# Pools for the first attention loads, joined attention outputs and stores, and pools for the output projection's first tiles, in a two-layer hybrid transformer

## The chip, the cores and the metric

The program runs on one core of a Trainium2 chip. The metric is device time in microseconds (us) of one execution, lower is better; the median over several executions stands for a kernel. One further execution is taken with the hardware profiler on.

## What is computed

Two layers of a diffusion backbone over 2048 latent tokens (a grid of 32 rows by 64 columns) and 256 context tokens, width 1024. Per layer, cut to what matters here:

```python
qa, ka, va, bx, bb, bc, qn, kn, vn = _split_last(h @ w_in[l], IN_SPLITS)
o_a = windowed_gqa_latent(rope(qa), rope(ka), va, ka_c, va_c, attn_sink[l])  # 6 heads on 2 kv heads, |dt| <= 128, context, sink
o_b = gated_short_conv(bx, bb, bc, conv_w[l])
o_c = neighbourhood_attention_latent(qn, kn, vn, kn_c, vn_c, na_rpb[l])      # 6 heads, 8 x 16 window, position bias, context
x_mid = ln_affine(ALPHA * x + g1 * (concat(o_a, o_b, o_c) @ w_out[l]), ln1_g[l], ln1_b[l])
x = ln_affine(ALPHA * x_mid + g2 * expert_choice_ffn(modulate(ln(x_mid))), ln2_g[l], ln2_b[l])
```

In layer 0 the context tokens pass through the same steps (their queries see the context keys alone); in layer 1 only their keys and values are needed. Head size is 64; all is float32, and every product is made of three matmuls on operands that are split into a high and a low part.

## The kernel before

A layer is four phases, each a function: `phase_in` (L510, modulation, layer norm, projection), `phase_att` (L901), `phase_out` (L1263, output projection, norm, router) and the experts. A phase opens its pools of tiles where the pools of the phase before have been closed, so a tile's first use waits for the last use of what lay at the same place. Weights go through a stream of their own, `W`: a raw tile is loaded (L163, SP queue), ScalarE makes the high part `wh` (L178), VectorE the low part `wl` (L186). The order of the work on each engine is the order in which the program is written, with generators that are stepped in turn.

`phase_in` works on chunks of four token tiles, of which the fifth (chunk 4, after chunks 0 to 3) has two. For each it makes the q and k of the windowed heads with rotary (`a_rest`, L757), v, then q and k of the neighbourhood heads (`c_rest`) and the short convolution (L679 to L731). High and low parts of q and k (tiles `sth`, `stl`, two buffers each) go to DRAM arrays QA, KA, QC, KC. These are laid out head by head, high and low under each head, so a tile of two heads (128 partitions) is stored by two DMAs of 64 partitions for each part: `a_rest` has eight stores to a token tile (L792, L793), `c_rest` four to a piece (L665), all on the SP queue. Between the pieces of chunk 4 stand rows of the modulation (L468 on VectorE, L469 on PE).

`phase_att` takes two kv heads of the windowed attention (A: 16 latent blocks of 128 queries, 3 q heads each; in layer 0 also two context blocks) and then six neighbourhood heads (C: 4 blocks of 16 columns; in layer 0 one block of context). A block's queries are loaded by three DMAs (L983, L987), keys of a head by one (L958). Each member of a block (a q head, or a quarter of a C block) goes through: logits (PE, L1068 and L1069), maximum with mask or bias (VectorE, L1090), exp (ScalarE, L1098), transposes (PE, L1115 and L1138), high part (ScalarE, L1227), low part (VectorE, L1218), and the product with v (PE, L1173). A block ends with a copy (ScalarE, L1179), transposes (PE, L1186), a copy (L1189), and on VectorE: the sink term (L1181, A only, with an exp on ScalarE in L1182), its addition to the sum (L1191, A only), the reciprocal (L1193), the sum of the two halves (L1195) and the multiplication with the reciprocal (L1198). Then `o` is stored: MIXA by one DMA (L1200), MIXC by four (L1206), the last block's by the POOL queue. The order inside a step is written out by hand (`ORDERA`, `ORDERC`, L47 and L48), the product with v trails by three members (`LAG`). GpSimd (POOL) builds the biases of the next C block (L1020 to L1032).

`phase_out` loads for each token tile `mix` (L1284 from MIXA, L1294 from MIXC) and the convolution's parts `mh`, `ml` (L1288), transposes `mix` (L1307), splits it (L1309, L1311) and multiplies by w_out (L1324). The SP queue runs in order: a DMA that waits for a buffer holds all behind it. Eight semaphores rotate over the DMAs of SP and ScalarE.

## Time and profile before

| | before |
|---|---|
| median of 3 runs | 4099.59 us (4097.3 to 4102.42) |
| the profiled execution, own time | 4102.85 us |
| its span in the profile | 4101.1 us |
| PE busy | 3784.8 us, 92% of the span |
| VectorE (DVE) busy | 2898.5 us, 71% |
| ScalarE (ACT) busy | 2005.5 us, 49% |
| GpSimd (POOL) busy | 711.5 us, 17% |

The span is first to last instruction; 1.75 us of the profiled execution lie outside. The first layer's attention runs from 616 to 1050 us, the second's from 2705 to 3104. Busy shares are means over phases that have different limits, so each phase is read by itself.

### The profile page before, as it was taken

Reading aid. Unit: us, or ns where it says so; the run is one execution under the profiler, and the core shown is the slowest. Engines: PE = TensorE matmul, PEld = TensorE weight load, DVE = VectorE, ACT = ScalarE, POOL = GpSimd, SP = SyncE. Lnnn points to the kernel's source line nnn. Section 1 sums busy time; section 2 is a strip of 40 time slices with the busy share of each in tenths; the row PEclk is TensorE's granted clock in tenths of the full one; section 3 lists DMA queues with packets and bytes.
Section 4 is the critical chain, followed back from the end, with each engine's and each line's share of the span. In section 5 each row is a group of like instructions: output and inputs, shape, how many; then the busy total and the mean of one; then the engine's idle time right before and its main releaser. Section 6 shows DMA issues by size and latency. Waiting matters only on the chain. (4 is left out here: it accounts for less than half of the span.)

```text
span 4101.1 us, 64178 instructions
## 1 busy us (share of the span) xinstructions
PE 3784.8 (92%) x22980; PEld 3241.1 (79%) x22980; DVE 2898.5 (71%) x5836; ACT 2005.5 (49%) x3918; POOL 711.5 (17%) x658
## 2 busy tenths in 40 slices
PE   7999999999898899999996999989998965999983
PEld 5887888888787378988985888889997855999972
DVE  6555558999677477777756766469996776777765
ACT  4344338988433044444433434359884332444453
POOL 0000000022132023233311100000221321222214
PEclk9999999999999999999998999999999977999996
DMA  7666665377643777777756766553676424888875
GB/s 228 174 210 197 197 187 146 97 174 183 211 159 122 212 240 218 218 218 214 207 167 221 229 194 196 174 167 108 150 175 230 162 106 153 247 247 254 254 236 183
DMA packets 768951, 785.81 MB, mean 192 GB/s; under 512 B 144912, under 2 KB 650520, under 8 KB 766584
## 3 DMA queue, kind: packets, MB, share of 16 engines
q1 hardware_dynamic: 732776, 657.53, 53.4%
q0 software_dynamic: 34704, 123.13, 10.8%
q8 instruction: 182, 2.98, 0.3%
q14 instruction: 137, 1.12, 0.1%
q10 hardware_dynamic: 1152, 1.05, 0.1%
HBM read 603.05 MB, written 178.48 MB: 191 GB/s over the span
## 5 line engine op out<-in xcount | busy, mean ns | idle before, releaser
L178 ACT CAST wh<-wraw 128x1024 fp32r<-128x1024 f32 x636 | 656.5, 1049 | 379.8 <-DMA wraw<-in_w_in 139.0
L186 DVE TENSOR_TENSOR wl<-wraw,wh 128x1024 fp32r<-128x1024 f32 x636 | 751.2, 1216 | 17.9 <-ACT wh L178 17.5
L1218 DVE TENSOR_TENSOR pl<-pt,ph 128x256 fp32r<-128x256 f32 (+2 forms) x792 | 360.4, 495 | 13.8 <-ACT ph L1227 7.9
L632 PE MATMUL gem<-hh,wh 128*128 128x512 f32 (+1 forms) x960 | 352.5, 367 | 0.1
L1098 ACT ACTIVATE p<-lg,mx 128x640 f32<-128x640 f32 (+3 forms) x408 | 332.0, 814 | 37.5 <-DVE mx L1090 35.7
L634 PE MATMUL gem<-hh,wl 128*128 128x512 f32 (+1 forms) x960 | 348.2, 363 | 0.0
L633 PE MATMUL gem<-hl,wh 128*128 128x512 f32 (+1 forms) x960 | 346.7, 361 | 0.0
L1227 ACT CAST ph<-pt 128x256 fp32r<-128x256 f32 (+2 forms) x792 | 309.0, 446 | 58.5 <-PE pt L1115 52.5
L1838 PE MATMUL pu<-xh,wh 128*128 128x288 f32 (+1 forms) x1024 | 303.1, 296 | 8.7 <-DVE sa L1666 8.7
L1838 PE MATMUL pa<-xh,wh 128*128 128x288 f32 (+1 forms) x1024 | 299.6, 293 | 0.7 <-DVE modc L424 0.7
L1068 PE MATMUL lg<-k,q 128*128 128x384 f32 (+2 forms) x768 | 280.4, 387 | 19.5 <-DMA maskA<-in_maskA 7.4
L1840 PE MATMUL pa<-xh,wl 128*128 128x288 f32 (+1 forms) x1024 | 296.0, 289 | 0.8 <-DVE wl L186 0.8
L1839 PE MATMUL pa<-xl,wh 128*128 128x288 f32 (+1 forms) x1024 | 295.6, 289 | 0.0
L1840 PE MATMUL pu<-xh,wl 128*128 128x288 f32 (+1 forms) x1024 | 295.3, 288 | 0.0
L1839 PE MATMUL pu<-xl,wh 128*128 128x288 f32 (+1 forms) x1024 | 295.1, 288 | 0.0
L1577 POOL DMA_INDIRECT xe<-H,ix x80 | 164.4, 2055 | 475.5 <-DVE ix L1572 398.6
L1700 POOL DMA_INDIRECT ACC<-y,ix x62 | 129.9, 2094 | 576.1 <-DVE y L1681 323.6
L1069 PE MATMUL lg<-k,q 128*128 128x256 f32 x816 | 228.7, 286 | 0.3 <-ACT p L1098 0.3
L1875 PE MATMUL py<-wh,gh 128*128 128x512 f32 x512 | 206.4, 403 | 18.4 <-ACT gh L1668 11.8
L810 PE MATMUL gem<-wh,hh 128*128 128x512 f32 x544 | 219.7, 404 | 1.2 <-ACT hh L601 1.2
L811 PE MATMUL gem<-wl,hh 128*128 128x512 f32 x544 | 216.1, 397 | 1.4 <-DVE wl L186 1.4
L812 PE MATMUL gem<-wh,hl 128*128 128x512 f32 x544 | 215.7, 396 | 0.0
(346 smaller groups left out, 9680.7 us busy)
## 6 DMA issues: line engine op xcount, KB each, us to landing
wraw<-in_w_in SPq DMA_DIRECT2D x160, 512.0 KB
wraw<-in_w_gate SPq DMA_DIRECT2D x128, 512.0 KB
wraw<-in_w_up SPq DMA_DIRECT2D x128, 512.0 KB
wraw<-in_w_down SPq DMA_DIRECT2D x128, 512.0 KB
wraw<-in_w_mod SPq DMA_DIRECT2D x88, 512.0 KB
vw<-VS SPq DMA_DIRECT2D x192, 128.0 KB
q<-QA SPq DMA_DIRECT2D x204, 96.0 KB
VS<-vs SPq DMA_DIRECT2D x36, 512.0 KB
```

Source lines behind the costliest of these rows:

```text
L178: self.nc.scalar.copy(h, self.raw[i])
L186: self.nc.vector.tensor_tensor(e[1], self.raw[i], e[0].bitcast(F32), op=ALU.subtract)
L632: P.matmul(pg[:, t0:nt], wh[:, cs_], hh[:, k, t0:nt], start=(k == 0), stop=False)
L633: P.matmul(pg[:, t0:nt], wh[:, cs_], hl[:, k, t0:nt], start=False, stop=False)
L634: P.matmul(pg[:, t0:nt], wl[:, cs_], hh[:, k, t0:nt], start=False, stop=(k == KD - 1))
L1068: P.matmul(pl[:, w0:512], q[:, x, m, :], win(k), start=(x == 0), stop=(x == 1))
L1098: S.activation(p[:, 0:768 - w0], rec["lg"][:, w0:768], AF.Exp, bias=st[b]["mx"][:, m:m + 1], scale=-1.0, accum_out=st[b]["ss"][:, m:m + 1])
L1218: V.tensor_tensor(view(st[b]["pl"]), src, view(st[b]["ph"].bitcast(F32)), op=ALU.subtract)
L1227: S.copy(view(st[b]["ph"]), src)
L1838: P.matmul(pp[f], wh[:, cs_], xh[:, kk, :], start=(kk == 0), stop=False)
L1839: P.matmul(pp[f], wh[:, cs_], xl[:, kk, :], start=False, stop=False)
L1840: P.matmul(pp[f], wl[:, cs_], xh[:, kk, :], start=False, stop=(kk == KD - 1))
```

## The change

1. QA, QC and KC are laid out part by part (high, low), then head by head, so a 128-partition tile is one store: four stores to a token tile in `a_rest`, two to a piece in `c_rest`. A head's keys are now loaded by two DMAs. In all, SP and ScalarE issue 2254 DMAs instead of 2544.
2. Pools: in `phase_in` the ring `hT` becomes `hodd` and `heven`, and the PSUM tiles `gem` get a pool. In `phase_att` nearly every tile has its own pool, in an order by which the first block's q, k, mask and v lie where tiles of earlier chunks were.
3. Outputs of up to four A blocks, or of two C blocks, share one tile for maximum, sum, reciprocal and `o`. The steps L1181, L1182, L1191, L1193, L1198 and the store run once per group. The multiplication of A moves to GpSimd.
4. In `phase_out` the tiles `mix`, `mh`, `ml` of the first three token tiles get pools that lie where the last head's work has nothing; PSUM is split in three pools.

```diff
-    QA = dr("QA", [6, 2, 64, TT])
+    QA = dr("QA", [2, 6, 64, TT])
     KA = dr("KA", [2, 2, 64, TT])
-    QC = dr("QC", [6, 2, 64, TT])
-    KC = dr("KC", [6, 2, 64, TT])
+    QC = dr("QC", [2, 6, 64, TT])
...
-        hp = es.enter_context(tc.tile_pool(name="hT", bufs=2))
+        hodd = es.enter_context(tc.tile_pool(name="hodd", bufs=1))
+        heven = es.enter_context(tc.tile_pool(name="heven", bufs=1))
         sb = es.enter_context(tc.tile_pool(name="in_sb", bufs=2))
         last = l == DEPTH - 1
-        hT = {-1: [hp.tile([128, KD, 512], F32R, name=z) for z in ("hh", "hl")]}
+        hT = {}
...
+        psg = es.enter_context(tc.tile_pool(name="in_psg", bufs=4, space=PSUM))
...
                 dst = QC[l] if f < 3 else KC[l]
                 for a, z in enumerate((sh, sl)):
-                    for b in range(2):
-                        SY.dma_start(dst[2 * (f % 3) + b, a, :, tok + t0:tok + nt],
-                                     z.bitcast(F32)[64 * b:64 * b + 64, t0:nt])
+                    SY.dma_start(dst[a, 2 * (f % 3):2 * (f % 3) + 2, :, tok + t0:tok + nt].rearrange("h d n -> (h d) n"),
+                                 z.bitcast(F32)[:, t0:nt])
...
                 for a, o in enumerate((qh, ql)):
-                    for b in range(2):
-                        z = o.bitcast(F32)[64 * b:64 * b + 64]
-                        SY.dma_start(QA[l][b::2, a, :, tk].rearrange("f p n -> p f n"), z[:, 0:3, :])
-                        SY.dma_start(KA[l][b, a, :, tk], z[:, 3, :])
+                    SY.dma_start(QA[l][a, :, :, tk].rearrange("(f b) p n -> (b p) f n", b=2), o.bitcast(F32)[:, 0:3, :])
+                    SY.dma_start(KA[l][a, :, :, tk].rearrange("h d n -> (h d) n"), o.bitcast(F32)[:, 3, :])
...
-        kp = es.enter_context(tc.tile_pool(name="at_k", bufs=2))
+        def pool(name, bufs=1, **kw):
+            return es.enter_context(tc.tile_pool(name=name, bufs=bufs, **kw))
+        qp = pool("at_q")
         shift(es, 64)
-        qp = es.enter_context(tc.tile_pool(name="at_q", bufs=1))
-        vwp = es.enter_context(tc.tile_pool(name="at_vw", bufs=3))
-        op = es.enter_context(tc.tile_pool(name="at_o", bufs=6))
-        mp = es.enter_context(tc.tile_pool(name="at_m", bufs=1))
-        vp = es.enter_context(tc.tile_pool(name="at_v", bufs=2))
-        sm = es.enter_context(tc.tile_pool(name="at_s", bufs=4))
-        pp = es.enter_context(tc.tile_pool(name="at_p", bufs=3))
+        kp = [pool("at_k0")]
+        mp = pool("at_m")
+        vp = [None, pool("at_v1")]
+        vp[0] = pool("at_v0")
+        pp = pool("at_p", 3)
+        sm = pool("at_s", 3)
+        hp = [pool("at_h0")]
+        lp = [pool("at_w0")]
+        hp.append(pool("at_h1"))
+        lp.append(pool("at_w1"))
         shift(es, 64)
-        hp = es.enter_context(tc.tile_pool(name="at_h", bufs=2))
-        wp = es.enter_context(tc.tile_pool(name="at_w", bufs=2))
-        bp = es.enter_context(tc.tile_pool(name="at_b", bufs=1))
-        psl = es.enter_context(tc.tile_pool(name="at_l", bufs=2, space=PSUM))
-        pst = es.enter_context(tc.tile_pool(name="at_t", bufs=3, space=PSUM))
-        pso = es.enter_context(tc.tile_pool(name="at_po", bufs=1, space=PSUM))
+        kp.append(pool("at_k1"))
+        op = pool("at_o", 3)
+        bsp = pool("at_bias")
+        tp = pool("at_toep", 2)
+        vwp = pool("at_vw", 3)
+        vxp = pool("at_vx", 2)
+        wp = pool("at_ot", 2)
+        bp = pool("at_b")
+        psl = [pool("at_l0", space=PSUM)]
+        pst = pool("at_t", 3, space=PSUM)
+        pso = pool("at_po", space=PSUM)
+        psl.append(pool("at_l1", space=PSUM))
...
+        group = {}
+        for kind, u in [("A", 0), ("A", 1)] + [("C", u) for u in range(6)]:
+            for rows in (range(2, 6), range(6, 10), range(10, 14), range(14, NT), (0, 1)) if kind == "A" else (
+                    ((4,), (0, 1), (2,), (3,)) if u == 5 else ((4,), (0, 1), (2, 3))):
+                for j, n in enumerate(rows):
+                    group[kind, u, n] = ((kind, u, rows[0]), j, len(rows))
...
-            src = (KA if kind == "A" else KC)[l][u].rearrange("a d n -> (a d) n")
-            k = r["k"] = kp.tile([128, TT], F32R, name="k")
+            src = (KA if kind == "A" else KC)[l][:, u]
+            k = r["k"] = kp[ulist.index((kind, u)) % 2].tile([128, TT], F32R, name="k")
...
-                SY.dma_start(k.bitcast(F32)[:, 128 * t0:128 * t1], src[:, 128 * t0:128 * t1])
+                for a in range(2):
+                    SY.dma_start(k.bitcast(F32)[64 * a:64 * a + 64, 128 * t0:128 * t1], src[a, :, 128 * t0:128 * t1])
...
-                st[b] = {z: sm.tile([128, 4], F32, name=z) for z in ("mx", "ss", "rs")}
+                g, j, ng = group[b]
+                if j == 0:
+                    st["of", g] = {z: sm.tile([128, 12], F32, name=z)[:, 0:ng * nm] for z in ("mx", "ss", "rs")}
+                st[b] = {z: x[:, j * nm:j * nm + nm] for z, x in st["of", g].items()}
...
-            if kind == "A":
-                V.tensor_tensor(rec["rs"][:, :nm], sink[:, 3 * u:3 * u + 3], rec["mx"][:, :nm], op=ALU.subtract)
-                S.activation(rec["rs"][:, :nm], rec["rs"][:, :nm], AF.Exp, scale=-1.0)
+            g, j, ng = group[b]
+            of = st["of", g]
+            end = j == ng - 1
+            if end and kind == "A":
+                V.tensor_tensor(of["rs"].rearrange("p (b m) -> p b m", b=ng),
+                                sink[:, None, 3 * u:3 * u + 3].to_broadcast([128, ng, 3]),
+                                of["mx"].rearrange("p (b m) -> p b m", b=ng), op=ALU.subtract)
+                S.activation(of["rs"], of["rs"], AF.Exp, scale=-1.0)
...
-            o = op.tile([128, 4, 64], F32, name="o")
-            S.copy(o[:, :nm, :], px[:, :nm, 64:128])
+            if j == 0:
+                of["o"] = op.tile([128, 12, 64], F32, name="o")[:, 0:ng * nm, :]
+            all_ = of["o"]
+            o = all_[:, j * nm:j * nm + nm, :]
+            S.copy(o, px[:, :nm, 64:128])
+            if end and kind == "A":
+                V.tensor_tensor(of["ss"], of["ss"], of["rs"], op=ALU.add)
+            yield
+            if end:
+                V.reciprocal(of["rs"], of["ss"])
+            yield
+            V.tensor_tensor(o, px[:, :nm, 0:64], o, op=ALU.add)
+            del st[b], blks[b]
+            if not end:
+                return
+            yield
+            yield
+            (G if kind == "A" else V).tensor_tensor(all_, all_, of["rs"][:, :, None].to_broadcast([128, ng * nm, 64]),
+                                                       op=ALU.mult)
+            n0 = g[2]
             if kind == "A":
-                V.tensor_tensor(rec["ss"][:, :nm], rec["ss"][:, :nm], rec["rs"][:, :nm], op=ALU.add)
-            yield
-            V.reciprocal(rec["rs"][:, :nm], rec["ss"][:, :nm])
-            yield
-            V.tensor_tensor(o[:, :nm, :], px[:, :nm, 0:64], o[:, :nm, :], op=ALU.add)
-            yield
-            yield
-            V.tensor_tensor(o[:, :nm, :], o[:, :nm, :], rec["rs"][:, :nm, None].to_broadcast([128, nm, 64]), op=ALU.mult)
-            if kind == "A":
-                SY.dma_start(MIXA[l][128 * n:128 * n + 128, 192 * u:192 * u + 192], o[:, 0:3, :].rearrange("p m d -> p (m d)"))
+                SY.dma_start(MIXA[l][128 * n0:128 * (n0 + ng), 192 * u:192 * u + 192].rearrange("(b p) c -> p b c", p=128),
+                             all_.rearrange("p (b m) d -> p b (m d)", b=ng))
             elif n == 4:
-                SY.dma_start(MIXC[l][0:256, 64 * u:64 * u + 64].rearrange("(m p) d -> p m d", p=128), o[:, 0:2, :])
+                SY.dma_start(MIXC[l][0:256, 64 * u:64 * u + 64].rearrange("(m p) d -> p m d", p=128), all_)
             else:
                 dst = MIXC[l][256:TT, 64 * u:64 * u + 64].rearrange("(m a g b) d -> m g a b d", m=4, a=8, g=4)
-                for m in range(4):
-                    (G if b == blist[-1] else SY).dma_start(dst[m, n], o[:, m, :])
-            del st[b], blks[b]
+                for x in range(ng):
+                    for m in range(4):
+                        (G if b == blist[-1] else SY).dma_start(dst[m, n0 + x], all_[:, 4 * x + m, :])
+            del st["of", g]
...
+        yp = es.enter_context(tc.tile_pool(name="out_y", bufs=1))
+        mp = [es.enter_context(tc.tile_pool(name=f"out_m{j}", bufs=1)) for j in range(3)]
         sb = es.enter_context(tc.tile_pool(name="out_sb", bufs=2))
         rows = es.enter_context(tc.tile_pool(name="out_rows", bufs=1))
-        ps = es.enter_context(tc.tile_pool(name="out_ps", bufs=2, space=PSUM))
+        pst = es.enter_context(tc.tile_pool(name="out_pt", bufs=2, space=PSUM))
+        ps = es.enter_context(tc.tile_pool(name="out_ps", bufs=1, space=PSUM))
+        pso = es.enter_context(tc.tile_pool(name="out_po", bufs=2, space=PSUM))
         last = l == DEPTH - 1
...
-            m = sb.tile([128, 768], F32, name="mix", bufs=3)
+            m = mp[n % 3].tile([128, 768], F32, name="mix")
...
-            mh = sb.tile([128, KD, 128], F32R, name="mh", bufs=3)
-            ml = sb.tile([128, KD, 128], F32R, name="ml", bufs=3)
+            mh = mp[n % 3].tile([128, KD, 128], F32R, name="mh")
+            ml = mp[n % 3].tile([128, KD, 128], F32R, name="ml")
```

Where this moves instructions. The SP queue, stores of one token tile of chunk 4 (first layer, `a_rest`), before and now:

```order
L792 DMA QA_80<-sth 64x3x128
L793 DMA KA_82<-sth 64x128
L792 DMA QA_80<-sth 64x3x128
L793 DMA KA_82<-sth 64x128
L792 DMA QA_80<-stl 64x3x128
L793 DMA KA_82<-stl 64x128
L792 DMA QA_80<-stl 64x3x128
L793 DMA KA_82<-stl 64x128
```

```order
L792 DMA QA_80<-sth 128x3x128
L793 DMA KA_82<-sth 128x128
L792 DMA QA_80<-stl 128x3x128
L793 DMA KA_82<-stl 128x128
```

The last store of a `sth` buffer moves from the fourth place to the second, that of an `stl` buffer from the eighth to the fourth.

VectorE in the steady part of A, one block of three members; before, and now in a block that does not end its group:

```order
L1195 TENSOR_TENSOR o<-pt,o 128x192
L1218 TENSOR_TENSOR pl<-pt,ph 128x3x128
L1218 TENSOR_TENSOR pl<-pt,ph 128x2x128
L1090 ISA lg,mx<-lg,maskA,sinks 128x640
L1090 ISA mx 128x1
L1198 TENSOR_TENSOR o<-o,rs 128x192
L1181 TENSOR_TENSOR rs<-sinks,mx 128x3
L1218 TENSOR_TENSOR pl<-pt,ph 128x3x128
L1218 TENSOR_TENSOR pl<-pt,ph 128x2x128
L1090 ISA lg,mx<-lg,maskA,sinks 128x640
L1090 ISA mx 128x1
L1191 TENSOR_TENSOR ss<-ss,rs 128x3
```

```order
L1228 TENSOR_TENSOR o<-pt,o 128x192
L1258 TENSOR_TENSOR pl<-pt,ph 128x3x128
L1258 TENSOR_TENSOR pl<-pt,ph 128x2x128
L1113 ISA lg,mx<-lg,maskA,sinks 128x640
L1113 ISA mx 128x1
L1258 TENSOR_TENSOR pl<-pt,ph 128x3x128
L1258 TENSOR_TENSOR pl<-pt,ph 128x2x128
L1113 ISA lg,mx<-lg,maskA,sinks 128x640
L1113 ISA mx 128x1
L1258 TENSOR_TENSOR pl<-pt,ph 128x3x128
L1258 TENSOR_TENSOR pl<-pt,ph 128x2x128
```

The multiplication, the sink term, the addition and (below the piece) the reciprocal are gone from three blocks of four. A group's multiplication stands on GpSimd as `L1234 TENSOR_TENSOR o<-o,rs 128x768`: eight of these in each layer, and two of 384 in layer 0.

ScalarE where attention ends and the projection begins (layer 0; behind "waits" stand the semaphores, DMAHW those of SP and ScalarE DMAs, DMASW those of the POOL queue), before and now:

```order
L1179 COPY ot<-po 128x512 [waits PE_49]
L1189 COPY o<-pt 128x256 [waits DMAHW2_49,DMAHW1_49,DMAHW3_49,DMAHW0_49,PE_49]
L178 CAST wh<-wraw 128x1024 [waits DVE_49,Activation_49,Pool_49]
L178 CAST wh<-wraw 128x1024
L1309 CAST mh<-pt 128x384 [waits DMAHW1_49,DMAHW0_49,DMAHW2_49,DMASW7_49,DMAHW3_49,DMASW6_49,DMAHW4_49,DMASW5_49,DMAHW5_49,DMASW0_49,DMAHW6_49,DVE_49,DMAHW7_49,PE_49,Activation_49]
```

```order
L1203 COPY ot<-po 128x512 [waits PE_49]
L1221 COPY o<-pt 128x256 [waits DMAHW7_49,PE_49]
L178 CAST wh<-wraw 128x1024 [waits DMAHW1_49,DMAHW0_49,DMAHW2_49,DMASW7_49,DMAHW3_49,DMASW6_49,DMAHW4_49,DMASW5_49,DMAHW5_49,DMASW0_49,DMAHW6_49,DVE_49,DMAHW7_49,Activation_49,Pool_49]
L178 CAST wh<-wraw 128x1024
L1354 CAST mh<-pt 128x384 [waits PE_49] x2
```

The wait for all stores of the last head has moved from the first `mix` load and the first `mh` to the first `wh` of w_out.

## Rows read from the trace of the kernel before

**Rows 1.** Stretch of the A part, layer 0: us, busy PE, PEld, DVE, ACT, POOL, PEclk, DMA share, GB/s.

```profile
640.00:700.00 60.00, 60.00 (x425) 55.55 (x424) 59.52 (x181) 54.60 (x159) 0.00 (x0) 1.00 0.47 141
```

**Rows 2.** Timeline, chunk 4 of layer 0: start, duration, engine, instruction, idle before and releaser.

```profile
580.22 0.61 SPq L793 DMA_DIRECT2D KA<-sth  x1
...
582.88 0.60 SPq L793 DMA_DIRECT2D KA<-stl  x1
...
583.41 0.37 ACT L653 CAST sth<-gem 128x256 fp32r<-128x256 f32 x1 [3.29 <-DMA KA<-sth]
...
585.01 0.42 DVE L655 TENSOR_TENSOR stl<-gem,sth 128x256 fp32r<-128x256 f32 x1 [4.57 <-DMA KA<-stl]
...
585.66 0.37 PE L469 MATMUL tr<-ident,mcols 128*24 128x128 f32 x1 [6.13 <-DVE mcols L468]
```

**Rows 3.** Timeline where projection ends and attention begins, layer 0; last row layer 1.

```profile
607.72 1.19 SPq L665 DMA_DIRECT2D KC<-stl  x2
616.38 1.93 SPq L983 DMA_DIRECT2D q<-QA  x3
...
617.74 0.36 ACTq L731 DMA_DIRECT2D OB<-stl  x1
...
623.49 0.55 PE L1068 MATMUL lg<-k,q 128*128 128x256 f32 x1 [7.15 <-DMA k<-KA]
...
625.11 0.76 DVE L1090 CUSTOM_DVE_ANT_0 lg<-lg,maskA,sinks 128x512 f32<-128x512 f32 x1 [7.40 <-DMA maskA<-in_maskA]
...
625.96 0.69 ACT L1098 ACTIVATE p<-lg,mx 128x512 f32<-128x512 f32 x1 [4.05 <-DVE mx L1090]
...
2715.08 1.28 ACT L1098 ACT_TABLE_LOAD   x1 [8.97 <-DMA q<-QA]
```

**Rows 4.** Timeline of VectorE in a block of A, layer 0.

```profile
699.73 0.35 DVE L1198 TENSOR_TENSOR o<-o,rs 128x192 f32<-128x192 f32 x1
700.00 0.15 DVE L1181 TENSOR_TENSOR rs<-sinks,mx 128x3 f32<-128x3 f32 x1
700.07 0.88 DVE L1218 TENSOR_TENSOR pl<-pt,ph 128x384 fp32r<-128x384 f32 x2
```

**Rows 5.** Timeline of PE in the same block.

```profile
700.74 0.38 PE L1138 MATMUL pt<-ident,p 128*128 128x128 f32 x2
701.05 0.44 PE L1068 MATMUL lg<-k,q 128*128 128x384 f32 x1
...
703.11 0.38 PE L1138 MATMUL pt<-ident,p 128*128 128x128 f32 x2
703.25 0.42 PE L1068 MATMUL lg<-k,q 128*128 128x384 f32 x1
```

**Rows 6.** Timeline of POOL and VectorE where a bias is built beside A, layer 0.

```profile
755.97 3.32 POOL L1032 TENSOR_TENSOR bias<-maskC,toep 128x384 f32<-128x384 f32 x3
...
757.13 1.22 DVE L1181 TENSOR_TENSOR rs<-sinks,mx 128x3 f32<-128x3 f32 x1
```

**Rows 7.** Waits of PE in C, layer 0, 850 to 1030 us: total, times, longest.

```profile
PE po L1173 <- ACT ot L1179: 3.9, 5, 0.8
PE pt L1138 <- DVE pl L1218: 2.3, 5, 0.5
```

**Rows 8.** Timeline where attention ends and the output projection begins, layer 0.

```profile
1046.17 2.40 SPq L1206 DMA_DIRECT2D MIXC<-o  x4
1054.55 0.34 SPq L1284 DMA_DIRECT2D mix<-MIXA  x1
...
1049.22 1.99 ACT L178 CAST wh<-wraw 128x1024 fp32r<-128x1024 f32 x2
1058.69 0.48 ACT L1309 CAST mh<-pt 128x384 fp32r<-128x384 f32 x1 [7.48 <-DMA mh<-OB]
...
1057.74 0.87 PE L1307 MATMUL pt<-ident,mix 128*128 128x128 f32 x3 [8.82 <-DMA ml<-OB]
...
1059.86 1.20 PE L1324 MATMUL po<-wh,mh 128*128 128x512 f32 x2
```

More of the change, by code (lines that the diff above doesn't have):

```diff
@@ L384, in build, with mod_piece @@
     mod_done = set()
-    def mod_piece(l, j, ps, sb, split=True, big="gem", nbig=4, small="tr", apart=False, room=None):
-        pm = ps.tile([128, 512], F32, name=big, bufs=nbig)
+    def mod_piece(l, j, ps, sb, split=True, big="gem", nbig=4, small="tr", apart=False, room=None, acc=None):
+        pm = (acc or ps).tile([128, 512], F32, name=big, bufs=nbig)
         n = 4 if split else 2
@@ L524, in prep @@
             ts = chunk_tiles(c)
-            hT[c] = [hp.tile([128, KD, 512], F32R, name=z) for z in ("hh", "hl")]
+            hT[c] = [(hodd if c % 2 else heven).tile([128, KD, 512], F32R, name=z) for z in ("hh", "hl")]
             groups = GROUPS[l] if c == 0 else [(b, 2, b * DELAY) for b in range(0, len(ts), 2)]
@@ L628, in s_piece @@
                 wh, wl = W.next(key)
-                pg = ps.tile([128, 512], F32, name="gem", bufs=4)
+                pg = psg.tile([128, 512], F32, name="gem")
                 for k in range(KD):
@@ L804, in one_tile @@
                     wait_for(c, j)
-                    pg = ps.tile([128, 512], F32, name="gem", bufs=4)
+                    pg = psg.tile([128, 512], F32, name="gem")
                     for k in range(KD):
@@ L818, in ctx_tiles @@
                     wait_for(c, 1)
-                    pg = ps.tile([128, 512], F32, name="gem", bufs=4)
+                    pg = psg.tile([128, 512], F32, name="gem")
                     for k in range(KD):
@@ L866, in phase_in @@
             for j in range(8):
-                next(mod_piece(0, FIRST[j], ps, mb, j % 2 == 1))
+                next(mod_piece(0, FIRST[j], ps, mb, j % 2 == 1, acc=psg))
                 T.tick()
@@ L924, in phase_att @@
         maskC = bp.tile([128, 3 * MWID], F32, name="maskC")
-        biases = [None, bp.tile([128, BWID], F32, name="bias")]
+        biases = [None, bsp.tile([128, BWID], F32, name="bias")]
         sink = sinks[:, l, :]
@@ L1054, in qk @@
             q = blks[b]["q"]
-            pl = psl.tile([128, 1024], F32, name="lg")
+            pl = psl[i % 2].tile([128, 1024], F32, name="lg")
             w0 = 512
@@ L1304, in tr @@
             for f in parts:
-                pt = ps.tile([128, 4, 128], F32, name="pt")
+                pt = pst.tile([128, 4, 128], F32, name="pt")
                 for j in range(3):
@@ L1347, in rest @@
             yield STEP
-            y = sb.tile([128, D], F32, name="y", bufs=3)
+            y = yp.tile([128, D], F32, name="y", bufs=3)
             for h in range(2):
@@ L1390, in rest @@
             yield STEP
-            lt = sb.tile([2 * NE, 128], F32, name="lt")
+            lt = yp.tile([2 * NE, 128], F32, name="lt", bufs=2)
             V.tensor_copy(lt, pr[:, 0:128])
@@ L1395, in rest @@
             P.matmul(pl[:, NE * i:NE * i + NE], lt, two, start=True, stop=True)
-        po = [ps.tile([128, D], F32, name="po") for _ in range(2)]
+        po = [pso.tile([128, D], F32, name="po") for _ in range(2)]
         for k in range(5):
@@ L1408, in phase_out @@
         SY.dma_start(wr32, k8(t["w_router"][l]))
-        wr = rows.tile([128, KD, 2 * NE], F32R, name="wr")
+        wr = yp.tile([128, KD, 2 * NE], F32R, name="wr")
         two = rows.tile([2 * NE, NE], F32, name="two")
@@ L1429, in phase_out @@
             if n >= 2:
-                po.append(ps.tile([128, D], F32, name="po"))
+                po.append(pso.tile([128, D], F32, name="po"))
             half = 4 if n >= 2 else 6
```

34 lines of the change are left out of this document (18 added, 16 removed).

## The prediction

> **What bounds the kernel now.** I read the busy shares by engine first, then the table of stretches, then for each place that the change touches the timeline and the list of waits, always asking what ends the idle time last. PE is busy for 92% of the span, so the kernel is a PE kernel with holes, and a change gains what it closes of the holes or, where another engine sets PE's pace, what it takes off that engine. The reader is to see four kinds of place.
>
> At three joints PE stands still. In chunk 4 of the projection it waits 6.13 us for a small copy on VectorE, which stands behind L655, and this one waits for the landing of the store KA<-stl [rows 2]. Where attention begins PE waits 7.15 us for the first keys: SP issued nothing between the last store at 607.72 + 1.19 and the first q load at 616.38, the moment at which the last projection matmul ended (623.49 - 7.15 = 616.34), because q's place was still in use [rows 3]. Where attention ends PE waits 8.82 us for `mix`, `mh`, `ml`, whose loads SP could issue only at 1054.55 [rows 8]. Layer 1 repeats all three.
>
> In the A part PE is busy for 60.00 of 60 us and VectorE for 59.52 [rows 1]: both are full, and which of them sets the pace has to be read from a block. PE's starts show it: between the transposes L1138 and the logits that follow lie 0.31 us at 700.74 and 0.14 at 703.11 [rows 5], so 0.17 us in a block is a wait that the busy time hides. It stands right behind VectorE's multiplication and sink term [rows 4]. VectorE sets the pace there, but PE has little left to win.
>
> In C no engine is full; PE's waits in 180 us of it are 3.9 us for ScalarE and 2.3 for VectorE, none for a DMA [rows 7].
>
> **The sum, term by term.** It is made against the profiled execution, 4102.85 us, which is 3.26 us above the median of the runs.
>
> *Chunk 4, -5 us.* SP's spacing is (582.88 - 580.22) / 4 = 0.66 us a store [rows 2]. The last store of `sth` goes from fourth to second place, 1.3 us earlier, that of `stl` from eighth to fourth, 2.7 earlier. L653 then starts near 582.1, L655 near 582.4 instead of 585.01, PE near 583.1 instead of 585.66: 2.6 us, in two layers 5. Bounds: if a 128-partition store is that much slower to land, 1 us a layer is left; more than the hole of 6.13 it cannot give. Taken: -5, between -2 and -12. In the other chunks the saved issues give nothing, since PE runs through.
>
> *Attention's start, -14 us.* The q load now asks only for transposes long done, and k for chunk 3's matmuls, so SP issues them behind the last KC store. That store is itself one DMA instead of two, and ends near 607.7 + 0.6 = 608.3. From issue to the first logits it took 623.49 - 616.38 = 7.1 us, to the mask 625.11 - 616.38 = 8.7 [rows 3]; one more issue for k adds 0.6. So keys are there at 616.0 and the mask near 617.6, both when PE ends the projection or little after. The next late thing is ScalarE: its last OB store ends at 617.74 + 0.36 = 618.10, then a table load of 1.28, so the first exp starts near 619.4 instead of 625.96: 6.6 us. In layer 1 the table load began 8.97 us after ScalarE's last work, at 2715.08; behind two OB issues (0.9 us by estimate, from 0.36 for one and the gap between them) it would begin 8.1 earlier. Sum 14.7; I take 14, as OB's issues may wait about a microsecond for a semaphore that the early loads hold. Bounds: -8 if the loads, beside the last stores, land 3 us later than they did alone; -17 if the table load falls into time in which ScalarE is idle anyway.
>
> *A part, -11 us.* In three blocks of four VectorE loses L1181 (700.00 to 700.07: 0.07) and its like L1191 and L1193 (taken at 0.07 each), in every block L1198 (699.73 to 700.00: 0.27) [rows 4]: 0.27 + 3/4 x 0.21 = 0.43 us a block. There are 64 latent blocks in the two layers: 28 us if VectorE alone sets the pace. PE's visible wait is 0.17 a block, 11 us. I take PE's value, since PE cannot run faster than its own instructions; the ends are 3 (a quarter of it) and 28. ScalarE loses only L1182 in three of four.
>
> GpSimd gets 18 multiplications. A 384-wide one takes 3.32 / 3 = 1.1 us [rows 6], so 768 is 2.2 by estimate. Nothing but a store waits for them: a group's output tile comes round again three groups later. What they can do is hold VectorE up: L1181, an operation of 0.15 us on three columns took 1.22 beside a GpSimd operation [rows 6]. [...] I count it at nothing, because the operations that are stretched in the row stand once per group now, and behind a group's multiplication comes a block without them [rows 4, 6]; what fills VectorE there, L1090 and L1218, reads PSUM.
>
> *C part, -3 us.* The two-block groups take one reciprocal and the fixed part of one multiplication from each pair. Of PE's 6.2 us of waits in 180 [rows 7] half may go in the first layer, little in the second. Bounds: -6 (all of the first layer's) and +3 (stores of eight at once, which hold q and v loads longer).
>
> *Output projection's start, -5.5 us.* The loads no longer wait: they issue behind SP's last store, at 1046.17 + 2.40 = 1048.57 instead of 1054.55, 6 us earlier [rows 8]. But the wait for the last head's stores has gone to ScalarE's first `wh` of w_out. Before, both casts lay hidden at 1049.22 [rows 8]. Now they begin when the last stores have landed, at 1054.55, where SP's load was released; 1.99 for both and 0.48 for `mh` [rows 8] put the first product near 1057.1 instead of 1059.86. That is 2.8 us a layer. Bounds: -2 in all if the POOL queue's stores land 2 us later than SP's release shows; -12 if the casts too wait for nothing.
>
> Sum: -5 - 14 - 11 - 3 - 5.5 = -38.5: the profiled execution near 4064, the median near 4099.6 - 38.5 = 4061.
>
> **The rivals.**
> - *VectorE alone sets A's pace* (28 for A, 6 for C): -58.5, 4041. For it: 59.52 of 60 [rows 1]. Against: PE's own wait is 0.17 [rows 5].
> - *A's pace does not move*, since ScalarE or PE's own chain follows at once (3 for A, 0 for C): -27.5, 4072. For it: PE 60.00 of 60 [rows 1].
> - *The first loads still wait*, as some pool lies differently than read: without attention's start and with nothing in the output projection but its own shift, -5 - 11 - 3 = -19, 4081.
> - *GpSimd locks VectorE out*: 16 x 2.2 + 2 x 1.1 = 37 us lost in A, so -1, 4098: no difference. For it: the stretched L1181 [rows 6]. [...]
> - *C's stores block its loads*: slower. There are 22 bursts of eight stores in the two layers; four more stores in a row hold SP for 2.4 us [rows 8]. If q and v loads had no lead over their use, each burst would cost PE that: 22 x 2.4 = 53, in all +14, 4114. It decides from the point at which the lead is under 2.4 us; no DMA among PE's waits [rows 7] speaks against it.
>
> **How the numbers follow.** Forecast 0.48 (alone it would be 4050 to 4070), A's pace unmoved 0.22, VectorE alone 0.12, loads still waiting 0.08, GpSimd 0.05, stores 0.05. The range runs from 4037, just below the case of VectorE alone, to 4082, above the case of waiting loads, and leaves out the last two and the far ends. A measurement of this kernel can tell about 0.2%, 8 us: the first four cases are faster, 0.90; GpSimd is no difference, 0.05; stores are slower, 0.05.
>
> **What would show it.** In the profile after: PE's hole in chunk 4 near 3.6 us; q loads issued before the last projection matmul and the first exp near 3.3 us after it; A's blocks 0.17 us shorter, with the pair of starts at L1138 as close after the first member as after the second; the multiplications on GpSimd without stretched operations on VectorE; `wh` of w_out cast some 5 us later than before, and the first product 2.8 us earlier. It is wrong if PE waits for q or v in C, if the first exp comes over 6 us after the last projection matmul, or if A's block time does not change.

## The result, and the profile after

The changed kernel is slower. Its median is 4132.94 us (4129.18 to 4136.26, 4 runs) against 4101.01 of the kernel before (4 runs): a ratio of 1.0072, 95% interval 1.0059 to 1.0086. The forecast was 4061, faster by 0.9%. The profiled execution took 4129.18 us, its span is 4127.4, 26.3 us more than before. The page's first lines:

```profile
span 4127.4 us, 63392 instructions
...
PE 3797.2 (92%) x22980; PEld 3245.8 (79%) x22980; DVE 2870.0 (70%) x5574; ACT 2004.1 (49%) x3868; POOL 732.2 (18%) x676
```

VectorE has 28 us less to do, as the joining promised, and nothing came of it. To see where the time went I cut both traces at the same events: a layer's last projection matmul, the transposes of the first output (L1186, in the changed kernel L1215), those of A's last block, those of the last C block, and the first and last product of the output projection (L1324, now L1369). Lengths in us, layer 0 and layer 1:

| stage | before | after | difference, both layers |
|---|---|---|---|
| projection | 508.9, 457.2 | 507.9, 455.1 | -3.1 |
| its end to the first output | 23.1, 25.1 | 16.4, 16.2 | -15.6 |
| A, first to last output | 187.0, 176.3 | 184.4, 173.7 | -5.2 |
| C, from there to the last output | 222.5, 195.6 | 238.2, 222.4 | +42.5 |
| last output to first product | 11.2, 11.4 | 12.6, 13.4 | +3.4 |
| output projection | 246.1, 218.9 | 249.6, 220.8 | +5.4 |
| all else | | | -1.1 |

The sum is +26.3. The first three gain 24 us; C alone loses 42.5.

**Attention's start** (timelines of the changed kernel; the last row is layer 1) answers to [rows 3]:

```profile
599.78 1.99 SPq L1003 DMA_DIRECT2D q<-QA  x3
...
617.42 1.28 ACT L1121 ACT_TABLE_LOAD   x1 [1.11 <-DVE stl L729]
618.72 0.69 ACT L1121 ACTIVATE p<-lg,mx 128x512 f32<-128x512 f32 x1
...
2714.26 0.69 ACT L1121 ACTIVATE p<-lg,mx 128x512 f32<-128x512 f32 x1
```

SP issues the first q 16.6 us earlier, and the first exp starts 3.6 us after the last projection matmul (615.13) instead of 9.9. **Chunk 4** answers to [rows 2]; the hole is 4.74 us instead of 6.13, and PE goes on 2.1 us earlier:

```profile
582.90 0.43 DVE L658 TENSOR_TENSOR stl<-gem,sth 128x256 fp32r<-128x256 f32 x1 [3.47 <-DMA KA<-stl]
...
583.56 0.37 PE L470 MATMUL tr<-ident,mcols 128*24 128x128 f32 x1 [4.74 <-DVE mcols L469]
```

**A** answers to [rows 1, 5]. VectorE is down from 59.52 to 57.72 us in 60, PE is as full as before, and the wait of 0.31 us between L1162 and the logits L1088 is still there. The stretch, then PE, then ScalarE in the same block:

```profile
640.00:700.00 60.00, 60.00 (x427) 55.42 (x426) 57.72 (x147) 54.33 (x153) 4.43 (x3) 1.00 0.52 138
```

```profile
692.92 0.38 PE L1162 MATMUL pt<-ident,p 128*128 128x128 f32 x2
693.23 0.44 PE L1088 MATMUL lg<-k,q 128*128 128x384 f32 x1
```

```profile
692.28 0.81 ACT L1121 ACTIVATE p<-lg,mx 128x640 f32<-128x640 f32 x1
692.97 0.21 ACT L1121 ACTIVATION_READ_ACCUMULATOR p<-lg,mx 128x1 f32 x1
```

The logits start 0.05 us after ScalarE has read out the sum of an exp (692.97 + 0.21 = 693.18), which frees one of two tiles of logits. Before the change it was the same 0.05 us: 700.79 + 0.21 = 701.00, and the logits of [rows 5] start at 701.05.

```profile
700.79 0.21 ACT L1098 ACTIVATION_READ_ACCUMULATOR p<-lg,mx 128x1 f32 x1
```

With the multiplication gone from VectorE the wait is as long as before, so it was not VectorE's multiplication that the logits waited for. A block fell from 5.69 to 5.66 us.

**C** in layer 1. VectorE's waits from 2905 to 3120 us, then GpSimd's (total, times, longest):

```profile
DVE lg L1113 <- POOL bias L1052: 12.0, 3, 5.4
...
DVE lg L1113 <- POOL va L1052: 8.9, 2, 5.0
```

```profile
POOL bias L1052 <- DMA toep<-in_rpb: 75.0, 3, 29.4
POOL va L1052 <- DMA toep<-in_rpb: 57.1, 2, 29.1
```

Five changes of head, five waits: VectorE waits for a bias that GpSimd builds, and GpSimd for the table `toep` of the next head. One of them, SP, then GpSimd, VectorE and PE:

```profile
2978.30 4.92 SPq L1246 DMA_DIRECT2D MIXC<-o  x8
...
2987.42 1.11 SPq L978 DMA_DIRECT2D k<-KC  x2
...
2989.27 0.66 SPq L991 DMA_DIRECT2D toep<-in_rpb  x1
```

```profile
3002.40 3.17 POOL L1052 TENSOR_TENSOR bias<-maskC,toep 128x384 f32<-128x384 f32 x3 [29.44 <-DMA toep<-in_rpb]
...
3003.43 0.83 DVE L1113 CUSTOM_DVE_ANT_0 lg<-lg,bias 128x640 f32<-128x640 f32 x1 [5.42 <-POOL bias L1052]
...
3004.92 0.69 PE L1162 MATMUL pt<-ident,p 128*128 128x128 f32 x2 [4.09 <-DVE pl L1258]
```

The same place before the change, which the rows ahead of the prediction do not show:

```profile
2981.94 0.45 SPq L958 DMA_DIRECT2D k<-KC  x1
...
2982.97 0.66 SPq L971 DMA_DIRECT2D toep<-in_rpb  x1
```

```profile
2993.13 3.52 POOL L1032 TENSOR_TENSOR bias<-maskC,toep 128x384 f32<-128x384 f32 x3 [22.11 <-DMA toep<-in_rpb]
...
2995.62 0.83 DVE L1090 CUSTOM_DVE_ANT_0 lg<-lg,bias 128x640 f32<-128x640 f32 x1 [0.22 <-PE lg L1069]
```

From issue to GpSimd's start the table took 10.2 us before and 13.1 after, and the first of GpSimd's three pieces (1.1 us) was done some 1.3 us before VectorE asked: that was the whole margin. The table is also issued later against the head's work: 9.9 us after the last output transposes of the head before (2972.9 + 0.2) in the kernel before, 13.6 after (2975.5 + 0.2). So it is issued 3.7 us later and takes 2.9 us longer; less the margin of 1.3 that is 5.3, and the wait is 5.42. The five waits come to 20.9 of the 26.8 us that C lost in layer 1. The rest stands mostly in the second block of a head (9.3 to 10.4 us instead of 8.3) and was not followed further.

**C** in layer 0 lost 15.7 us in another way. VectorE waits only 1.6 us for a bias there, but PE waits for queries. PE's waits from 825 to 1050 us, where the kernel before had none for a DMA [rows 7], and the longest of them, SP, then PE:

```profile
PE lg L1088 <- DMA q<-QC: 7.3, 4, 4.6
```

```profile
962.26 4.95 SPq L1246 DMA_DIRECT2D MIXC<-o  x8
...
967.76 4.01 SPq L1009 DMA_DIRECT2D q<-QC  x6
```

```profile
971.74 0.41 PE L1088 MATMUL lg<-k,q 128*128 128x384 f32 x1 [4.56 <-DMA q<-QC]
```

The queries stand in SP's queue behind eight joined stores, which hold it for 5 us.

**The projection's start** answers to [rows 8]. PE, then ScalarE, then the issue-to-landing time of the POOL queue's four stores before and after:

```profile
1056.68 0.55 PE L1352 MATMUL pt<-ident,mix 128*128 128x128 f32 x3 [2.35 <-DMA mix<-MIXA]
...
1066.66 1.19 PE L1369 MATMUL po<-wh,mh 128*128 128x512 f32 x2 [6.79 <-ACT mh L1354]
```

```profile
1064.19 1.99 ACT L178 CAST wh<-wraw 128x1024 fp32r<-128x1024 f32 x2 [9.46 <-DMA xr<-in_ctx]
```

```profile
MIXC<-o POOLq DMA_DIRECT2D x4, 32.0 KB, 2.0
```

```profile
MIXC<-o POOLq DMA_DIRECT2D x4, 32.0 KB, 4.8
```

The loads are early, but the stores that ScalarE's first cast waits for are now in flight beside them and land in 4.8 us instead of 2.0: from 1056 to 1064 the DMA engines are busy for 0.43 to 1.05 of each us at 120 to 402 GB/s, where before the change, from 1050 to 1055, it was 0 to 0.27 at up to 63 GB/s. The row of the cast names another load (xr) as what came last; that it is the stores is read from the program's list of waits, from the trace, where the last of the four lands at 1063.97, 0.2 us ahead of the cast, and from e4 below.

### The profile page after: what moved, and what is told of

The parts are those of the page before. It is cut to its first block, busy times and chain, and to the rows that moved or that the text cites. A ratio compares the mean times of both kernels' runs of the same rounds, so it can differ in the third digit from the quotient of the medians.

```text
span 4127.4 us, 63392 instructions
## 1 busy us (share of the span) xinstructions
PE 3797.2 (92%) x22980; PEld 3245.8 (79%) x22980; DVE 2870.0 (70%) x5574; ACT 2004.1 (49%) x3868; POOL 732.2 (18%) x676
## 3 DMA queue, kind: packets, MB, share of 16 engines
q10 hardware_dynamic: 1152, 1.05, 0.1%
## 5 line engine op out<-in xcount | busy, mean ns | idle before, releaser
L1258 DVE TENSOR_TENSOR pl<-pt,ph 128x256 fp32r<-128x256 f32 (+2 forms) x792 | 361.0, 496 | 27.4 <-ACT ph L1267 12.5
L1121 ACT ACTIVATE p<-lg,mx 128x640 f32<-128x640 f32 (+3 forms) x408 | 332.2, 814 | 40.3 <-DVE mx L1113 38.5
L1088 PE MATMUL lg<-k,q 128*128 128x384 f32 (+2 forms) x768 | 281.1, 387 | 17.9 <-ACT p L1121 9.3
```

What stands on the lines that cost most here:

```text
L1088: P.matmul(pl[:, w0:512], q[:, x, m, :], win(k), start=(x == 0), stop=(x == 1))
L1121: S.activation(p[:, 0:768 - w0], rec["lg"][:, w0:768], AF.Exp, bias=st[b]["mx"][:, m:m + 1], scale=-1.0, accum_out=st[b]["ss"][:, m:m + 1])
L1258: V.tensor_tensor(view(st[b]["pl"]), src, view(st[b]["ph"].bitcast(F32)), op=ALU.subtract)
```

## The experiments

All numbers at a glance (medians beside the median of the kernel before in the same job; C and "start" are the stages above, layer 0 and 1, from each run's trace; e7 leaves out a part of the computation):

| run | median | before | ratio (95%) | C | start |
|---|---|---|---|---|---|
| change | 4132.9 | 4101.0 | 1.0072 (1.0059 to 1.0086) | 238.2, 222.4 | 12.6, 13.4 |
| e1_kone | 4100.5 | 4105.1 | 0.9992 (0.9982 to 1.0001) | 224.0, 208.9 | 13.4, 13.1 |
| e2_cst1 | 4134.4 | 4105.1 | 1.0075 (1.0058 to 1.0092) | 232.6, 234.0 | 13.1, 13.1 |
| e3_both | 4111.8 | 4105.1 | 1.0018 (1.0008 to 1.0027) | 222.0, 220.2 | 12.9, 12.9 |
| e4_swapo | 4115.7 | 4105.1 | 1.0028 (1.0019 to 1.0038) | 235.9, 222.2 | 5.3, 5.5 |
| f5_kone_swapo | 4091.2 | 4103.8 | 0.9971 (0.9960 to 0.9981) | 224.1, 213.9 | 5.5, 7.6 |
| f6_early | 4081.2 | 4103.8 | 0.9949 (0.9929 to 0.9969) | 224.9, 197.1 | 5.2, 9.9 |
| f7_c1_six | 4088.0 | 4103.8 | 0.9964 (0.9952 to 0.9976) | 221.8, 196.2 | 12.6, 13.1 |
| g1_before_halves | 4116.1 | 4103.5 | 1.0025 (1.0016 to 1.0035) | 222.3, 210.0 | 11.3, 11.1 |
| e8_toep | 4133.8 | 4103.5 | 1.0067 (1.0051 to 1.0084) | 243.0, 224.6 | 12.6, 12.6 |
| e7_nopl | 4105.0 | 4103.5 | 1.0006 (0.9997 to 1.0016) | 233.9, 224.0 | 13.1, 13.4 |
| e6_mulv | 4136.6 | 4103.8 | 1.0081 (1.0062 to 1.0101) | 236.2, 222.2 | 12.9, 13.4 |
| f8_best | 4072.3 | 4103.5 | 0.9922 (0.9905 to 0.9938) | 221.8, 196.8 | 5.4, 5.7 |
| f9_outm | 4077.6 | 4106.1 | 0.9933 (0.9917 to 0.9950) | 221.7, 198.7 | 7.2, 7.2 |
| f10_early_six | 4073.5 | 4106.1 | 0.9921 (0.9905 to 0.9938) | 221.7, 195.1 | 5.8, 10.6 |

**One load of keys.** The theory to test was "halves" against "queue". The diff is shortened; with the layout, the stores of KC go back to two of 64 partitions.

```diff
-    KC = dr("KC", [2, 6, 64, TT])
+    KC = dr("KC", [6, 2, 64, TT])
...
-                for a in range(2):
-                    SY.dma_start(k[64 * a:64 * a + 64, ...], src[a, ...])
+                SY.dma_start(k[:, ...], KC[l][u].rearrange("a d n -> (a d) n")[...])
```

> Only the layout of KC goes back, so that a neighbourhood head's keys are again one load of 128 partitions (and its stores two of 64). In the changed kernel VectorE waits some 5.4 us at nearly every change of head in layer 1 for a bias, whose table (toep) is issued 3.7 us later than before and lands 2.9 us slower. Theory 'halves' (two half loads of keys hold the DMA engines and the table behind them): landing back near 10 us, stall from 5.4 to under 2, the C part of layer 1 from 222 us to about 204, the median near 4100. Theory 'queue' (eight joined stores stand ahead of the table's issue): only the one issue of 0.66 us is won, C near 219, median near 4126.

It gave 32 us, as "halves" expected, and C 224.0 and 208.9. In layer 0 PE no longer waits for a DMA. In layer 1, C is still 13 us longer than before, so this is not all of it: the table takes 11.5 to 12.6 us there, not the 10 that was expected, and VectorE's longest wait is 4.9 us, not under 2. (In the change the five waits were 2.7 to 5.4 us, not 5.4 at nearly each as the expectation has it.)

**Stores of C one by one**, alone and with the single key load.

```diff
-   ((4,), (0, 1), (2,), (3,)) if u == 5 else ((4,), (0, 1), (2, 3))
+   ((4,), (0,), (1,), (2,), (3,))
```

> Only the groups of the neighbourhood blocks go back to one block each: four stores in a row instead of eight, reciprocal and multiplication per block. Theory 'queue': the table is issued about 3 us earlier against the block's work, stall from 5.4 to 2 or 3 us, C of layer 1 from 222 to about 208, median near 4108. Theory 'halves': the landing stays at 13 us, C stays above 216, median above 4122.

> Both of the two edits before together. If both causes add up and there is no third, C returns to its lengths of before (218 and 195 us against 234 and 222), and the median falls by some 43 us to about 4090. If a third cause in C remains (another pool, vx, order of POOL's work), it stays above 4105.

By their letter e2 came out as "halves" had it (C above 216, median above 4122) and e3 as its third cause (above 4105), but the reason is one that neither had named. Alone the edit won nothing; with the key load it was 11 us slower than the key load by itself. ScalarE's waits in C of layer 1 of e3 say why:

```profile
ACT o L1227 <- DMA MIXC<-o: 18.9, 5, 4.6
```

The pool `at_o` of the change has three buffers, enough for groups of two blocks; single blocks had six before. The edit brought a new wait of its own, and says nothing of the queue. f7 below mends it.

**The cast behind the stores.**

```diff
-        kp.append(pool("at_k1"))
         op = pool("at_o", 3)
+        kp.append(pool("at_k1"))
```

> Only the places of the pools at_o and at_k1 are exchanged, so that the first wh of w_out lies on the last-but-one place of keys instead of on outputs, and ScalarE's first cast doesn't wait for the POOL queue's four stores, which land 5.7 us after the last issue in the changed kernel. Theory 'stores under loads' (the early loads slow those stores, and the cast waits for them): first product some 8 us after the last transposes of attention instead of 12.6 and 13.4, median 8 to 10 us lower, near 4124. Rival: the first product waits for the loads of mix and of the convolution's parts anyway, which come no earlier: no change, 4132.

The first product comes 5.3 and 5.5 us after attention, a gain of 7.3 and 7.9, and the median fell by 17. ScalarE casts at 1052.27, right behind its last copy:

```profile
1052.27 1.99 ACT L178 CAST wh<-wraw 128x1024 fp32r<-128x1024 f32 x2
```

**Both mends together, and the rest of C.**

> The single key load and the exchanged places of at_o and at_k1 together, joined stores kept. They touch different places, so the gains of the two runs (32 and 17 us against the changed kernel) should add: median near 4084, C of layer 1 near 209 us, the first product some 5.4 us after the last transposes of attention. If instead an earlier projection only moves a wait to w_out's loads, less than 8 of the 17 remain.

4091.2: the gains add to within 8 us; 2 us of that came off the projection's start in layer 1 and 5 off C, where it is 213.9 against 208.9 in e1. Why C is longer was not followed.

> As f5, but a neighbourhood head's keys and table are issued one block earlier, ahead of the eight joined stores of the head before (its vx behind the table). Theory 'queue' for what is left in C of layer 1 (209 against 196 before): the table lands before VectorE asks, C of layer 1 196 to 199, of layer 0 222 or less, median near 4070. Rival: the rest is not the table's issue (the outputs' ring, the order on GpSimd): C stays near 209, median 4084.

```diff
-  if at == ustart[kind, u] + (4 if kind == "A" else 1) and x < len(ulist):
+  if at == ustart[kind, u] + (4 if kind == "A" else 0) and x < len(ulist):
```

(Shortened: the order of `vx` and the table is exchanged too.) C of layer 1 is 197.1: what was left there was the table's issue behind the eight stores, as "queue" says. Layer 0 did not move (224.9). The median is 11 us above the expectation; 2.3 of them stand in the projection's start in layer 1 (9.9), which the earlier loads made later and which was not followed.

> As f5, with the neighbourhood blocks stored one by one again, now from six output buffers of their own as before the change (the run with single groups had only three, and ScalarE waited there for MIXC stores). Theory 'queue': without eight stores in a row C of layer 1 is 196 to 200 us, median near 4072; and the 12 us by which single groups were slower than joined ones came from three buffers. Rival: single groups cost in themselves: C above 209.

```diff
+        ocp = pool("at_oc", 6)
...
-  of["o"] = op.tile([128, 12, 64], F32, name="o")[:, 0:ng * nm, :]
+  of["o"] = (op.tile(...) if kind == "A" else ocp.tile([128, 4, 64], F32, name="oc"))[:, 0:ng * nm, :]
```

C is 221.8 and 196.2, its length before the change; so the joined stores did cost the rest, and three buffers had hidden it. The new buffers lie under the first `wh`, so the projection's start is late again (12.6, 13.1): 12.6 us more than in f5, most of the 16 by which the median missed. f8 places them elsewhere.

**Half loads in the kernel before.** This is the suspected cost by itself:

> The kernel before, with nothing changed but that a neighbourhood head's keys are loaded as two DMAs of 64 partitions instead of one of 128. Theory 'halves': the table behind them lands some 3.5 us later, against a margin of 1.4 us in the trace of before, so VectorE waits about 2 us at most changes of head: C of layer 1 from 195.6 to about 204, of layer 0 from 222.5 to 226 or more, the time 10 to 15 us over before. Rival: half loads hurt only together with the joined stores: at most 4 us.

12.6 us slower, all in layer 1 (C 195.6 to 210.0), with the same wait as in the change:

```profile
DVE lg L1093 <- POOL bias L1035: 10.6, 3, 4.5
DVE lg L1093 <- POOL va L1035: 3.5, 2, 2.1
```

The five tables of layer 1 that GpSimd waits for took 9.8 to 10.5 us from issue to GpSimd in the kernel before, 12.0 to 12.7 here, and 13.1 to 13.9 in the change.

**The table ahead of the keys.** The lines that load `toep` stand before those that load `k`.

> The changed kernel with the table (toep) issued ahead of the two half loads of keys instead of behind them. Theory 'halves': the table no longer stands behind the slow loads, VectorE's wait for the bias in layer 1 shrinks from 5.4 to about 1 us, C of layer 1 from 222 to 203 to 208; if the keys are then late, PE waits for k<-KC in its place. Rival: the table is late because of its own issue or its own transfer: C above 217.

The median did not move, and C is 224.6 where 203 to 208 was expected. What came is the clause on the keys: VectorE's wait is gone, but PE waits for the keys; from 2890 to 3110 us:

```profile
PE lg L1089 <- DMA k<-KC: 20.6, 5, 5.7
```

So the table is not slow by itself: behind half loads it took 12.0 to 12.7 us in g1, behind one load 9.8 to 10.5 in the kernel before, and here, ahead of the half loads, VectorE has no wait for what is made from it, while PE waits up to 5.7 us for the keys. The order only says who is late.

**What paces A.**

> The changed kernel without the products of A's low parts of p with v (left out of the computation; VectorE still makes the low parts): some 0.8 us less of PE in each block of A. Theory 'PE sets the pace of A now': the block falls from 5.67 us toward VectorE's need of about 5.2, A from 184.4 and 173.7 us to about 170 and 159, median near 4105. Theory 'VectorE or ScalarE still sets it': A within 2 us of where it is, median near 4130.

```diff
-  for x, (w, s, c0, c1) in enumerate(steps):
+  for x, (w, s, c0, c1) in enumerate(steps if kind == "C" else []):
```

A fell by 6.8 and 8.5 us (177.6, 165.2), a block from 5.66 to 5.37: between the two expectations. The median fell by 28 us, of which these are 15. So PE's work paces A, but of the 0.8 us taken from it in a block (an estimate; in the trace of the change a block has five such products, 0.17 us from the start of one to the next start) only 0.3 came through, as the others follow at once; in 50 us PE, VectorE and ScalarE are then busy for 49.05, 48.55 and 47.46:

```profile
640.00:690.00 50.00, 49.05 (x325) 40.99 (x323) 48.55 (x132) 47.46 (x134) 3.67 (x3) 1.00 0.53 140
```

> The changed kernel with the multiplication of A back on VectorE, still once per group: some 0.2 us more of VectorE in each block of A, nothing on GpSimd there. Theory 'PE sets the pace of A': A stays within 1 us of 184.4 and 173.7 us, median near 4133. Theory 'VectorE sets it': some 6 us more in each layer, near 4145. Theory 'GpSimd's multiplications hold VectorE up': A shorter, below 4128.

```diff
-  (G if kind == "A" else V).tensor_tensor(all_, ...)
+  V.tensor_tensor(all_, ...)
```

4136.6 us, A 188.4 and 176.9: 4.0 and 3.2 us more. The block in which the multiplication falls takes 6.02 us instead of 5.66, the other three are as they were. That lies between the first two theories: VectorE has no room for a long operation at once. By A's lengths the move to GpSimd is worth 7 us and does no harm there; the two medians alone, a ratio of 1.0081 against 1.0072, could not tell it.

**The best version**, and two runs on what was left.

> Everything that the runs so far ask for: one key load, neighbourhood blocks stored one by one from six buffers that lie where the weight stream's first tile does not, at_o and at_k1 exchanged, and one PSUM pool in the output projection as before. C near 222 and 196 us, first product some 5.4 us after attention in both layers, the projection's tile at 13.95 us instead of 14.13 if the PSUM pools made that difference: median near 4070, some 0.8% under before. Rival for the last: the tile stays at 14.13, 4075.

4072.3 us, 0.78% faster than the kernel before (interval 0.62 to 0.95%), with every stage as expected but one: the output projection is 248.9 and 221.7 us, so its PSUM pools are not why it grew.

> As f8, but mix, mh and ml lie in one ring with the norm's tiles again, as before the change (its pools no longer lie apart). If their places in SBUF make the projection's tile 14.13 us instead of 13.95, the tile is 13.95 again and the projection 246 and 219 us; their first loads wait for more, so the first product comes later (11 us after attention instead of 5.4). Rival: the tile stays at 14.13, so it is something else (the tiles of y, the weights' ring).

4077.6: the projection is 249.7 and 221.0, so the places of `mix`, `mh` and `ml` are not why either. They are worth little besides: without pools of their own the first product comes 7.2 us after attention, with them 5.4 and 5.7. What lengthens the projection stays open.

> As f8 (but three PSUM pools), with a neighbourhood head's keys and table issued one block earlier, in front of the last blocks' stores. In f8 C is already at its length of before (221.8 and 196.8 us), so the table's margin, not its lateness, should grow: C within 1 us, median within 3 us of 4072. If something of C still hung on the table, C falls below 220 and 195.

4073.5, C 221.7 and 195.1: the median is as expected. The 1.7 us that C of layer 1 gains come with a projection's start that is 4.9 us later there (10.6), so no more is to be had this way.

## Why the prediction was wrong

**C, -3 forecast, +42.5 measured: the step that failed.** The sum has the half loads of keys only in the term on attention's start, as "one more issue for k adds 0.6"; in C they were put at nothing, without a reason. C's bounds went to +3 for stores of eight in a row. I held the queue's lead to be safe because PE's list of waits in C, in layer 0 alone, named no DMA [rows 7]. A wait that is not there says nothing of how much time is to spare. In layer 1 the margin lay two steps behind PE, where GpSimd waits for a table with 1.3 us to spare; that wait cost nothing before, so it stood in no list of PE or VectorE. In layer 1 the two causes add: half loads alone 14.4 us (g1), joined stores alone 13.3 (e1) to 18.3 (f5), both 26.8. In layer 0 either alone costs at most 1.6 (g1, e1, f5), both 15.7. There each head has an extra block of context, which should give the table more time (no run tests this), and what is late is the queries: PE waits for them in the runs with half loads and joined stores (7.3 us in the change, 4.0 in e4, 7.9 in e8), and not in g1, e1 or f5. The 7.3 us are not all of the 15.7; ScalarE waits another 3.2 us for a store of A's outputs (MIXA) at the first change of head, and the rest was not followed.

Why half loads are slow was not measured apart from this kernel. What stretches of 3 us, taken shortly behind the keys' issue in layer 1, show is that the DMA engines are as busy and move less; before, after, and in g1:

```profile
2983.00:2986.00 3.00, 3.00 (x25) 2.81 (x24) 2.98 (x8) 2.54 (x8) 0.00 (x0) 1.00 0.97 303
```

```profile
2990.00:2993.00 3.00, 3.00 (x25) 2.85 (x24) 2.85 (x7) 2.87 (x8) 0.00 (x0) 1.00 1.06 229
```

```profile
2990.00:2993.00 3.00, 3.00 (x24) 2.86 (x23) 2.71 (x6) 2.43 (x7) 0.00 (x0) 1.00 1.06 221
```

The last two columns are the share and the GB/s: 303 against 229 and 221. In g1 only the keys' loads differ from the kernel before. Other transfers are in these rows too, so they do not give the rate of a half load alone, and why less is moved is not shown.

**The rival on the slower side** (C's stores block its loads, 0.05, 4114) named the place and half of the mechanism. It expected q and v to be late, at 2.4 us a burst. In layer 0 PE did wait for q behind a burst of eight stores, 7.3 us in four waits, and that is one of the signs of being wrong that the prediction set itself. But the stores alone did not do it (e1, f5), and in layer 1 it was the table, at changes of head only. The half loads are missing in this rival too.

**Output projection's start, -5.5 forecast, +3.4 measured.** I saw that ScalarE's cast would wait for the last stores, and took 1054.55 [rows 8] as their landing. That was their landing without company. The same early loads that the change makes possible are in flight with the stores (DMA share up to 1.05 instead of 0.27); the stores' median landing went from 2.0 to 4.8 us, and the cast began at 1064.19, 10 us after SP's first load. e4 confirms the wait: without it the first product comes 7 us earlier than in the change (5.3 against 12.6) and 6 us earlier than before it (11.2).

**A, -11 forecast, -5.2 measured.** The step "VectorE sets the pace there" was wrong: the 0.17 us that I gave to VectorE's multiplication is by the rows above a wait for ScalarE's exp to free a tile of logits, and it is still there. The rival "A's pace does not move" (3 us) was nearer. Half of what was won lies in two blocks, one in each layer, that took 7.07 and 6.96 us and now 5.68: in each a sink term was stretched to 1.22 us [rows 6]. Now the longest in layer 0 is 0.37:

```profile
L1208 DVE TENSOR_TENSOR rs<-sinks,mx x10: 162/166/367, 646.5 to 813.5; 128x12 f32<-128x12 f32 x8, 128x6 f32<-128x6 f32 x2
```

```profile
L1234 POOL TENSOR_TENSOR o<-o,rs x9: 832/1475/1477, 650.9 to 810.1; 128x768 f32<-128x768 f32 x8, 128x384 f32<-128x384 f32 x1
```

So the rival "GpSimd locks VectorE out" fell: the multiplications (1.48 us, not the 2.2 of the estimate) stretch nothing. What falls beside the 18 in the trace is the maximum and the low parts, which read PSUM, and they take as long as elsewhere in attention (medians: L1113 with 640 columns and mask 885 ns against 884, L1258 with 384 columns 550 against 558, with 256 columns 417 against 415). In the kernel before it was the same beside GpSimd's bias pieces (L1218 with 256 columns 415 ns, as elsewhere). What these stretched there, the two sink terms (1.22 us against 0.16) and the multiplication L1198 (192 columns, median 0.76 against 0.36), has no counterpart beside any of the 18.

**What was right.** Attention's start gave 15.6 us against 14, by the steps named (q issued behind the last stores, the table load of ScalarE as the next late thing, the first exp 3.6 us after the projection against 3.3 forecast). Chunk 4 gave a hole of 4.74 us where 3.6 was said, and 3.1 us in all against 5: PE goes on 2.1 us earlier where the sum said 2.6, and in layer 0 one of these was lost again before the projection's end, which no run traced. The output projection's 5.4 us were in no term, and their cause is open.

Put together, -38.5 was forecast; the terms other than C came to -16, the change of sign is C's.

## What to carry to other kernels

A change that joins or splits DMAs moves what stands behind them in the queue (here the table of C, issued 3.7 us later): before pricing it, find the load with the smallest margin between landing and use, on whatever engine that is, and not only the loads that somebody waits for now. Saving stores by a layout that splits loads is no saving where the loads have less time to spare (here 1.3 us for the table; half loads alone made the program 12.6 us slower, g1). And where a pool's place is changed to free one engine early, read from the built program what the next tenant of the old place now waits for, and reckon that wait under the new traffic.

## What was not expected of the hardware

Two 512-column matmuls of the output projection take 0.46 us together before and 0.47 after (medians 0.457 to 0.460, and 0.467), with PE busy and the granted clock at 1.00; in the change, then before:

```profile
1157.45 0.63 PE L1369 MATMUL po<-wh,mh 128*128 128x512 f32 x2
1157.91 0.63 PE L1369 MATMUL po<-wl,mh 128*128 128x512 f32 x2
1158.38 0.39 PE L1369 MATMUL po<-wh,ml 128*128 128x512 f32 x1
```

```profile
1150.63 0.62 PE L1324 MATMUL po<-wh,mh 128*128 128x512 f32 x2
1151.09 0.62 PE L1324 MATMUL po<-wl,mh 128*128 128x512 f32 x2
1151.54 0.39 PE L1324 MATMUL po<-wh,ml 128*128 128x512 f32 x1
```

Over a token tile that is 14.13 us against 13.95, and the table above has 5.4 us for the whole program. Neither the PSUM pools (f8) nor the places of the stationary tiles (f9) bring it back; the cause is open.
